# First quarter of the first feed-forward product wholly by block products, its two halves in turn, products chained in PSUM banks

## The chip, the cores and the metric

The kernel runs as one program on one core of a Trainium2 chip. The core has a matrix engine (PE in the profile, with its weight loads as PEld), a vector engine (DVE), a scalar engine (ACT), GpSimd (POOL) and a queue that issues most loads (SP). The metric is the device time of one execution in microseconds, here the median of several runs; lower is better. Fp32 products are made from three matmuls on rounded parts: each operand is split into a high part (a cast on ACT) and the rest, the low part (a subtraction on DVE), and high×high, high×low and low×high are added up in PSUM.

## The reference

One encoder layer over 512 frames of width 1024. What the change touches is the feed-forward part at its end, above all its first product, u2 (512×1024) by `w_ff1` (1024×4096):

```python
        h = h + merged @ w_out[l]
        u2 = rmsnorm(h, g_ffn[l])
        h = h + jnp.square(jax.nn.relu(u2 @ w_ff1[l])) @ w_ff2[l]
    return rmsnorm(h, g_final)
```

## The kernel before

**Tiling.** The 4096 columns of the first product are cut into four quarters of 1024, each quarter into two halves (i = 0 and 1) of 512. For each quarter the kernel makes the first product, then the part of the second product (by `w_ff2`) that it feeds, and keeps the sums in the residual tiles `hN`. The frames are cut into two blocks of 256, and the 1024 rows of `w_ff1` into two blocks of 512, so that a half is a product of 2×2 blocks.

**Block products.** Such a half is made with seven block products instead of eight (Strassen's scheme in Winograd's form, numbered 1, 2, 5, 6, 3, 7, 4 in the order of `FIRST`). A block product is 24 matmuls of 256 columns: two column groups `a`, four `k`, three parts. Its left factors are sums of blocks of u2: products 1, 2 and 4 take plain blocks; 5, 6 and 7 take three sums kept in `u2sh`/`u2sl` (high and low part, slots 0, 1 and 2), and 3 takes a sum that goes by the tiles `R7` into slot 1 of `u2h`/`u2l`. Its right factors are blocks of weights (products 1, 2, 3) or sums of blocks, `tsum` (T1 to T4), which POOL's queue writes to device memory early in the program. That queue is paced: one step of these sums goes out behind each cast of a weight chunk from the twelfth on (`next_sum`).

**The first quarter before.** Half 0 of quarter 0 is made without block products: four tiles of 128 columns, each 24 matmuls of 512 columns' worth. Tiles 0 and 1 are made by 256 frames at a time (`half`), between and behind the transposes that turn the normalized rows into u2 (`u2_turn`, for four groups of 128 frames), tiles 2 and 3 in one piece (`plain_tile`). Meanwhile `u2_sums` makes the sums of u2 blocks. Half 1 is then made with the seven block products by `first_product`. In the other quarters both halves are, one after the other.

**Buffers.** Weight chunks (128×1024, 512 KB) come through `ring`: SP loads them into `raw` (three buffers in the pool `wp` and every fourth in `yp`), `split_b` casts them to `hi` on ACT and subtracts to `lo` on DVE (three buffers each). A buffer is written again when PE has finished with what it held. Results of block products go to PSUM tiles `mm` (four banks, each 128×512), are taken out by `first_evac` into `ev` and `od` (two tiles of 128×2×512 for each half), squared after a Relu (`relu2`), and split into `ch`/`cl` (`left`), the factors of the second product.

**Order.** PE's instructions run in the order of the code. The other engines' order is set by the scheduler when the program is built; `tc.issue_after(x)` puts an instruction behind x in it. `norm_end` is the last split of u2 on DVE.

## Time and profile before

| | |
|---|---|
| median of 3 runs | 816.25 us (816.25 to 816.32) |
| the profiled execution | 815.97 us, its span 814.2 us |
| PE busy | 805.0 us, 99% of the span |
| DVE busy | 590.2 us, 72% |
| ACT busy | 438.7 us, 54% |
| mean granted PE clock | 0.998 |

The span runs from the first to the last instruction; the 1.8 us between it and the execution's time lie around it. A row of the timeline gives start, duration, engine, line, operation, the tiles written and read, and the shape; "xN" merges N like instructions, and a bracket at the end tells how long the engine was idle before and what ended that. In the windows, each engine's busy time in a stretch stands with its count of instructions, then PE's granted clock, the busy share of the DMA engines, and GB/s.

### The profile page before, as it was taken

Reading aid. Unit: us, or ns where it says so; the run is one execution under the profiler, and the core shown is the slowest. Engines: PE = TensorE matmul, PEld = TensorE weight load, DVE = VectorE, ACT = ScalarE, POOL = GpSimd, SP = SyncE. Lnnn points to the kernel's source line nnn. Section 1 sums busy time; section 2 is a strip of 40 time slices with the busy share of each in tenths; the row PEclk is TensorE's granted clock in tenths of the full one; section 3 lists DMA queues with packets and bytes.
Section 4 is the critical chain, followed back from the end, with each engine's and each line's share of the span. In section 5 each row is a group of like instructions: output and inputs, shape, how many; then the busy total and the mean of one; then the engine's idle time right before and its main releaser. Section 6 shows DMA issues by size and latency. Waiting matters only on the chain.

```text
span 814.2 us, 12430 instructions
## 1 busy us (share of the span) xinstructions
PE 805.0 (99%) x4788; PEld 707.4 (87%) x4788; DVE 590.2 (72%) x913; ACT 438.7 (54%) x694; POOL 103.9 (13%) x127
## 2 busy tenths in 40 slices
PE   9999999999999999999999999999999999999996
PEld 7788888888888888999999889988998899889984
DVE  6857877546455587877567548896788778887896
ACT  7755655443344234444454536774676367637764
POOL 0000110011101212143143000011001100100011
PEclk9999999999999999999999999999999999999999
DMA  9433666688788867757755505878658855895543
GB/s 358 172 116 131 204 165 201 188 240 246 204 250 264 230 215 190 178 151 207 205 131 159 203 1 179 261 160 216 244 165 198 218 216 166 196 253 195 156 84 124
DMA packets 38604, 155.53 MB, mean 191 GB/s; under 512 B 4560, under 2 KB 5008, under 8 KB 36496
## 3 DMA queue, kind: packets, MB, share of 16 engines
q1 hardware_dynamic: 27424, 95.98, 32.8%
q0 software_dynamic: 9328, 54.01, 31.4%
q10 hardware_dynamic: 1792, 4.75, 1.6%
q8 instruction: 37, 0.61, 0.3%
q14 instruction: 23, 0.19, 0.1%
HBM read 152.58 MB, written 31.49 MB: 226 GB/s over the span
## 4 chain that ended last, share of the span: by engine, by line
PE 96%; DVE 1%; issue 1%; DMA 0%; ACT 0%; POOL 0%; POOLq 0%; DVEq 0%; ACTq 0%
PE mm L157 24%; PE mm L158 24%; PE mm L159 24%; PE a L157 5%; PE a L158 5%; PE a L159 5%; PE mm L380 1%; PE a L394 1%; PE a L624 1%; PE a L662 1%; PE a L661 1%; DVE h L1267 1%; PE a L900 1%; PE a L408 1%; DMA mem_s<-in_memT_dram 0%
## 5 line engine op out<-in xcount | busy, mean ns | idle before, releaser
L148 DVE TENSOR_TENSOR wlo<-raw,whi 128x1024 fp32r<-128x1024 f32 x67 | 86.4, 1293 | 58.9 <-ACT whi L147 58.7
L157 PE MATMUL mm<-uhi,whi 128*128 128x512 f32 (+1 forms) x352 | 125.9, 358 | 0.0
L159 PE MATMUL mm<-uhi,wlo 128*128 128x512 f32 (+1 forms) x352 | 123.7, 351 | 0.0
L158 PE MATMUL mm<-ulo,whi 128*128 128x512 f32 (+1 forms) x352 | 123.6, 351 | 0.0
L147 ACT CAST whi<-raw 128x1024 fp32r<-128x1024 f32 x67 | 70.4, 1051 | 92.9 <-PE mm L158 56.0
L1271 ACT CAST hi<-raw 128x1024 fp32r<-128x1024 f32 x65 | 68.2, 1049 | 49.7 <-PE mm L158 32.7
L1273 DVE TENSOR_TENSOR lo<-raw,hi 128x1024 fp32r<-128x1024 f32 x65 | 79.5, 1224 | 17.6 <-ACT hi L1271 17.6
L157 PEld LDWEIGHTS mm<-uhi,whi 128*128 128x128 f32 x352 | 66.7, 189 | 9.9 <-issue 1.5
L159 PEld LDWEIGHTS mm<-uhi,wlo 128*128 128x128 f32 x352 | 66.6, 189 | 9.1
L158 PEld LDWEIGHTS mm<-ulo,whi 128*128 128x128 f32 x352 | 66.7, 189 | 8.1
L1271 ACT CAST hi<-b 128x1024 fp32r<-128x1024 f32 x40 | 41.9, 1048 | 42.0 <-PE mm L159 25.6
L158 PE MATMUL mm<-u2l,hi 128*128 128x256 f32 x224 | 63.4, 283 | 0.0
L159 PE MATMUL mm<-u2h,lo 128*128 128x256 f32 x224 | 63.4, 283 | 0.0
L157 PE MATMUL mm<-u2h,hi 128*128 128x256 f32 x224 | 63.4, 283 | 0.0
L1457 POOL DMA_DIRECT2D b<-in_wst_dram x32 | 27.3, 853 | 271.3 <-DVE lo L1273 208.1
L1273 DVE TENSOR_TENSOR lo<-b,hi 128x1024 fp32r<-128x1024 f32 x40 | 48.9, 1224 | 14.1 <-ACT hi L1271 14.0
L158 PE MATMUL mm<-lo,ch 128*128 128x512 f32 x136 | 52.9, 389 | 0.0
L157 PE MATMUL mm<-hi,ch 128*128 128x512 f32 x136 | 52.9, 389 | 0.0
L159 PE MATMUL mm<-hi,cl 128*128 128x512 f32 x136 | 52.9, 389 | 0.0
L158 PE MATMUL mm<-u2sl,hi 128*128 128x256 f32 x168 | 47.5, 283 | 0.0
L157 PE MATMUL mm<-u2sh,hi 128*128 128x256 f32 x168 | 47.5, 283 | 0.0
L159 PE MATMUL mm<-u2sh,lo 128*128 128x256 f32 x168 | 47.5, 283 | 0.0
(414 smaller groups left out, 2093.2 us busy)
## 6 DMA issues: line engine op xcount, KB each, us to landing
raw<-in_wst_dram SPq DMA_DIRECT2D x114, 512.0 KB
b<-in_wst_dram POOLq DMA_DIRECT2D x32, 512.0 KB, 5.3
raw<-T SPq DMA_DIRECT2D x28, 512.0 KB
T<-in_wst_dram POOLq DMA_DIRECT2D x12, 1024.0 KB, 9.3
b<-in_wst_dram SPq DMA_DIRECT2D x16, 512.0 KB
wb<-in_wst_dram POOLq DMA_DIRECT2D x15, 512.0 KB, 5.3
wb<-in_wst_dram SPq DMA_DIRECT2D x8, 512.0 KB
nFb<-dF ACTq DMA_DIRECT2D x6, 512.0 KB
```

The costliest lines, as they stand in the source:

```text
L147: cast = nc.scalar.copy(hi, raw)
L148: low_now[0] = nc.vector.tensor_tensor(lo, raw, f(hi), op=ALU.subtract).ins
L157: nc.tensor.matmul(ps, lh, rh, start=start, stop=False, skip_group_check=on)
L158: nc.tensor.matmul(ps, lh, rl, start=False, stop=False, skip_group_check=on)
L159: nc.tensor.matmul(ps, ll, rh, start=False, stop=stop, skip_group_check=on)
L380: nc.tensor.matmul(kps[h], w[:, h * P:(h + 1) * P], x[:, k, :], start=k == p == 0, stop=k == KT - 1 and p == 2)
L394: nc.tensor.matmul(ps, x[:, k, sl], w[low][:, kk, :], start=k == low == 0 and x is mxh, stop=k == KT - 1 and low == 1)
L408: nc.tensor.transpose(pt[:, t * P:(t + 1) * P], xn[:, t, k * P:(k + 1) * P], ident)
L624: nc.tensor.matmul(ps[e], q[a, sl], k[a, :w], start=p == 0, stop=p == 2)
L1271: nc.scalar.copy(hi, raw)
L1273: nc.vector.tensor_tensor(lo, raw, f(hi), op=ALU.subtract)
L1457: nc.gpsimd.dma_start(to[i], wst[index["B", q, i, x]], accum_op=ALU.add)
```

## The change

Half 0 of the first quarter is made with block products as well, and the two halves alternate: product 1 of half 0, of half 1, product 2 of half 0, and so on, in every quarter. I call these blocks 1a, 1b, 2a, 2b, 5a, 5b, 6a, 6b, 3a, 3b, 7a, 7b, 4a, 4b (product, then a for half 0, b for half 1). Each half has two PSUM banks, x and y. Products 1, 6, 7 and 4 are added up in x, products 2 starts y, product 5 starts it anew and 3 is added to it; the sums that DVE made one by one before are now left in PSUM, and the evacuation reads x between two products. To make the additions right, the sum of u2 for product 6 takes the other sign (and the piece `R7`, made from it, is an addition now).

1a and 2a use the two weight chunks that were loaded early for tiles 0 and 1, and stand where `half` stood; the split of u2 that only the plain tiles needed (the first 512 rows for frames 256 to 511) goes away. `first_quarter` writes out the order of splits, sums and evacuations for the start. Where it passes `low_last`, all 16 matmuls that read the high part of a chunk come first, and the eight that read the low part last. The weight sums of quarter 0 now cover both halves, so eight steps on POOL's queue move 1024 KB instead of 512 KB.

```diff
-    L += [("T", "w_ff1", P * j) for j in range(4)]
...
-    tsum = {(n, q): dram.tile([2 if q else 1, P, 1024], F32, name=f"T{n}_{q}") for q in range(4) for n in (1, 2, 3, 4)}
+    tsum = {(n, q): dram.tile([2, P, 1024], F32, name=f"T{n}_{q}") for q in range(4) for n in (1, 2, 3, 4)}
...
+        def first_mms(n, w, ps, low_last=False):
+
+            wh, wl = (t.rearrange("p (a k c) -> p a k c", a=2, k=4) for t in w)
+            (uh, ul), s = U2[n]
+
+            def mm(a, k, x, y, start, stop):
+                nc.tensor.matmul(ps[:, a, :], x[:, a, k, :], y[:, s, k, :], start=start, stop=stop, skip_group_check=True)
+
+            for low in range(1 + low_last):
+                for a in range(2):
+                    for k in range(4):
+                        if not low:
+                            mm(a, k, wh, uh, n in (1, 2, 5) and a == k == 0, False)
+                            mm(a, k, wh, ul, False, False)
+                        if low or not low_last:
+                            mm(a, k, wl, uh, False, a == 1 and k == 3)
+                        yield
...
         u2_turn(2)
-        half(0, 0)
-        half(1, 0, range(4))
+        run(first_mms(1, ws[0], banks[0][0]))
+        rest = first_mms(2, ws[1], banks[0][1])
+        run(islice(rest, 4))
         norm_end = u2_turn(3)
-        half(1, 0, range(4, KT))
-        half(0, 1)
-        half(1, 1)
+        run(rest)
...
+        def first_evac(n, i, bank, after=None):
+
+            x, y = (ps.rearrange("p a t -> p (a t)") for ps in bank)
+            (a11, a21), (a12, a22) = ([z[i][:, h, :] for h in range(2)] for z in (ev, od))
             if n == 2:
-                nc.vector.tensor_tensor(a11, a21, ps, op=ALU.add)
+                nc.scalar.copy(a11, y)
+                with tc.issue_after(after) if after is not None else ExitStack():
+                    after = add(a11, x)
                 relu2(a11)
                 left(i, 0, a11)
             if n == 5:
-                nc.scalar.copy(a22, ps)
-            if n == 6:
-                sub(a21, a21, ps)
-                sub(a22, a22, a21)
+                nc.scalar.copy(a22, y)
             if n == 3:
-                nc.vector.tensor_tensor(a12, a22, ps, op=ALU.add)
+                nc.scalar.copy(a12, y)
+                after = sub(a12, a12, x)
                 relu2(a12)
                 left(i, 1, a12)
             if n == 7:
-                sub(a22, a22, ps)
-                add(a21, ps)
+                after = sub(a22, a22, x)
                 relu2(a22)
             if n == 4:
-                add(a21, ps)
-                relu2(a21)
+                nc.scalar.activation(a21, x, AF.Relu)
+                nc.scalar.activation(a21, a21, AF.Square)
                 late_left(i)
...
+            v = first_block(0, 1, 1, B, norm_end, True)
+            with tc.issue_after(v):
+                v = sub(a22, a21, a22)
+            v = first_block(0, 2, 1, B, v, True)
+            v = parts([x[:, 0] for x in u2s], a22, v)
+            v = first_evac(2, 0, A, v)
+            v = first_block(0, 5, 0, A, v, True)
+            first_evac(5, 0, A)
+            with tc.issue_after(v):
+                sub(a21, a11, a21)
+                v = sub(a11, a22, a11)
+            v = first_evac(2, 1, B, v)
+            v = first_block(0, 5, 1, B, v, True)
+            first_evac(5, 1, B)
+            v = parts([x[:, 1] for x in u2s], a11, v)
+            v = first_block(0, 6, 0, A, v)
+            for k in range(2):
+                sl = slice(512 * k, 512 * k + 512)
+                with tc.issue_after(v):
+                    v = nc.vector.tensor_tensor(R7[k], a12[:, sl], a11[:, sl], op=ALU.add).ins
+                    v = parts([x[:, 1, 2 * k:2 * k + 2, :] for x in u2], R7[k], v)
+            v = first_block(0, 6, 1, B, v)
+            v = first_block(0, 3, 0, A, v)
...
+        def first_product(q):
+
+            pair = banks if q == 0 else banks_of()
+            done = [None] * 3 if q else first_quarter()
+            for n in FIRST[0 if q else 5:]:
+                for i, bank in enumerate(pair):
+                    first_block(q, n, i, bank, done[-3])
+                    done.append(first_evac(n, i, bank))
...
-        plain_evac(0, first[0])
-        plain_evac(1, first[1])
-        plain_tile(2)
-        u2_sums()
-        plain_tile(3)
-        load_blocks(0)
-        first_product(0, 1)
-        second_product(0)
-        for q in range(1, NQ):
-            first_product(q, 0)
-            load_blocks(q)
+        for q in range(NQ):
+            first_product(q)
...
-            first_product(q, 1)
             second_product(q)
```

Two places show how the order of the built program changes. The first is DVE's queue from the last split of u2 on. Before, the splits of the two plain tiles (`wlo`) and of block product 1 come first, then the sums of u2 blocks (`b`, `R7`) with their low parts (`u2sl`, `u2l`):

```order
L148 TENSOR_TENSOR wlo_740_4925<-raw_738_4922,whi_739_4924 128x1024
L148 TENSOR_TENSOR wlo_745_4970<-raw_743_4967,whi_744_4969 128x1024
L1273 TENSOR_TENSOR lo_750_5018<-raw_748_5015,hi_749_5017 128x1024
L1264 TENSOR_TENSOR b121_4417<-b120_4416,b121_4417 128x1024
L1264 TENSOR_TENSOR b120_4416<-b110_4414,b120_4416 128x1024
L1264 TENSOR_TENSOR b110_4414<-b110_4414,b121_4417 128x1024
```

With the change DVE has, from the chunk of 5b (`lo_749`) to that of 6b (`lo_755`):

```order
L1289 TENSOR_TENSOR lo_749_4977<-raw_747_4974,hi_748_4976 128x1024
L210 TENSOR_TENSOR cl0_4860<-ev0_4852,ch0_4858 128x512
L210 TENSOR_TENSOR u2sl_4865<-b110_4414,u2sh_4864 128x1024
L1289 TENSOR_TENSOR lo_752_5010<-raw_750_5007,hi_751_5009 128x1024
L1381 TENSOR_TENSOR R70_4862<-b111_4415,b110_4414 128x512
L210 TENSOR_TENSOR cl1_4861<-ev1_4853,ch1_4859 128x512
L210 TENSOR_TENSOR u2l_4403<-R70_4862,u2h_4402 128x512
L1381 TENSOR_TENSOR R71_4863<-b111_4415,b110_4414 128x512
L210 TENSOR_TENSOR u2l_4403<-R71_4863,u2h_4402 128x512
L1289 TENSOR_TENSOR lo_755_5046<-raw_753_5043,hi_754_5045 128x1024
```

The sums of u2 blocks now stand between the splits of weight chunks that PE takes one after the other, and the low part for 6b stands behind both pieces of `R7`.

The second place is ACT's queue in the same stretch, from the high part of 6b's chunk (`hi_754`) on. The names `u2sh` stand for two casts: the first is of the sum for product 7 (`b120`), the second for product 6 (`b110`). `hi_757` and `hi_760` are the chunks of 3a and 3b, and `hi_760` takes the buffer that `hi_751`, the chunk of 6a, had:

```order
L1287 CAST hi_754_5045<-raw_753_5043 128x1024
L209 CAST ch0_4858<-ev0_4852 128x512
L209 CAST u2sh_4864<-b120_4416 128x1024
L1328 COPY od0_4854<-mm_723_4701 128x512
L209 CAST u2sh_4864<-b110_4414 128x1024
L1302 ACTIVATE ev1_4853<-ev1_4853 128x512
L1287 CAST hi_757_5075<-raw_756_5073 128x1024
L1303 ACTIVATE ev1_4853<-ev1_4853 128x512
L1328 COPY od1_4855<-mm_725_4703 128x512
L209 CAST ch1_4859<-ev1_4853 128x512
L209 CAST u2h_4402<-R70_4862 128x512
L1287 CAST hi_760_5117<-raw_759_5115 128x1024
```

Right behind that row follows the cast of the second piece of `R7`. Before, these casts had their place while PE worked on the plain tiles, and the second piece stood ahead of the cast for the block product that follows:

```order
L210 CAST u2h_4402<-R70_4912 128x512
L1304 ACTIVATE ev0_4902<-sq_742_4953 128x2x256
L210 CAST ch0_4908<-ev0_4902 128x512
L210 CAST u2h_4402<-R71_4913 128x512
L1271 CAST hi_757_5089<-raw_756_5087 128x1024
```

So the cast of the second piece has moved from ahead of a weight chunk's cast to behind one.

More of the change, by code (lines that the diff above doesn't have):

```diff
@@ L57, in chunk_list @@
         L += [("N", "w_out", 2 * j, 512 * c) for j in range(4)]
-    L += [("T", "w_ff1", P * j) for j in range(4)]
     for q in range(4):
-        L += [(kind, q, i, b) for kind in "FB" for b in ("11", "21", "12", "22") for i in range(2) if kind == "B" or q or i]
+        L += [(kind, q, i, b) for kind in "FB" for b in ("11", "21", "12", "22") for i in range(2)]
     return L
@@ L1207, in hybrid_block @@
         run(islice(c1, 24))
-        ws = [[t.rearrange("p (k c) -> p k c", k=KT) for t in own_w(("T", "w_ff1", P * j))] for j in range(2)]
+        ws = [own_w(("F", 0, 0, b)) for b in ("11", "21")]
         def u2_turn(t):
@@ L1272, in split_b, with ring @@
             with tc.issue_after(after) if after is not None else ExitStack():
-                nc.vector.tensor_tensor(lo, raw, f(hi), op=ALU.subtract)
+                low_now[0] = nc.vector.tensor_tensor(lo, raw, f(hi), op=ALU.subtract).ins
             return hi, lo
         load_n = [0]
-        def ring(src):
+        def ring(src, after=None):
             load_n[0] += 1
@@ L1281, in ring @@
             nc.sync.dma_start(raw, src)
-            return split_b(raw)
+            return split_b(raw, after)
         def relu2(x):
@@ new lines, in first_block, with first_quarter, parts @@
+        def first_block(q, n, i, bank, after=None, low_last=False):
+            if n in (1, 2, 3):
+                src = wst[index["F", q, i, {1: "11", 2: "21", 3: "22"}[n]]]
+            else:
+                src = tsum[{5: 1, 6: 2, 7: 3, 4: 4}[n], q][i]
+            w = ring(src, after)
+            low = low_now[0]
+            run(first_mms(n, w, bank[n in (2, 5, 3)], low_last))
+            return low
+        def first_quarter():
+            (a11, a12), (a21, a22) = b11, b12
+            A, B = banks
+            def parts(pair, src, after):
+                with tc.issue_after(after):
+                    return split(*(x.rearrange("p k t -> p (k t)") for x in pair), src)
+            v = first_block(0, 1, 1, B, norm_end, True)
[21 more added lines that the diff above has]
+            v = first_block(0, 3, 0, A, v)
+            done = [first_evac(3, 0, A)]
+            v = parts([x[:, 2] for x in u2s], a21, v)
+            load_blocks(0)
+            first_block(0, 3, 1, B, v)
+            return [None, *done, first_evac(3, 1, B)]
@@ L1387, in finish @@
+        def first_product(q):
[5 more added lines that the diff above has]
+                    done.append(first_evac(n, i, bank))
+                if n == 6:
+                    load_blocks(q)
         def finish(t, c, n):
```

76 lines of the change are left out of this document (11 added, 65 removed).

## The prediction, on record before the result

> **What bounds the kernel now.** I read the page's engine shares and the shares of its chain first, then the waits of PE, then PE's timeline at the edited place, and last the other engines' windows.
>
> ```profile
> PE 805.0 (99%) x4788; PEld 707.4 (87%) x4788; DVE 590.2 (72%) x913; ACT 438.7 (54%) x694; POOL 103.9 (13%) x127
> ...
> PE 96%; DVE 1%; issue 1%; DMA 0%; ACT 0%; POOL 0%; POOLq 0%; DVEq 0%; ACTq 0%
> ...
> PE a L290 <- DVE warm L287: 1.2, 1, 1.2
> PE mm L380 <- ACT hi L274: 0.5, 1, 0.5
> ```
>
> PE is busy 99% of the span and makes 96% of the chain; its two listed waits, 1.7 us together, belong to the program's start. So a matmul less is time less, unless something makes PE wait where it now does not. Whether there is room for that is told by the first feed-forward quarter:
>
> ```profile
> 495.81 0.28 PE L157 MATMUL mm<-u2h,f2h 128*128 128x256 f32 x1
> 501.57 0.40 PE L157 MATMUL mm<-u2h,whi 128*128 128x512 f32 x1
> 512.48 0.28 PE L157 MATMUL mm<-u2h,hi 128*128 128x256 f32 x1
> 532.63 0.40 PE L157 MATMUL a<-hi,ch 128*128 128x512 f32 x1
> ...
> 500.00:550.00 50.00, 50.00 (x308) 45.12 (x307) 44.60 (x55) 36.11 (x51) 5.14 (x6) 1.00 0.82 226
> 550.00:600.00 50.00, 50.00 (x337) 46.42 (x336) 36.78 (x43) 29.04 (x38) 3.40 (x4) 1.00 0.74 216
> ```
>
> The first four rows are where the shape of the work changes: 48 matmuls of 256 columns from 495.81 (0.120 us each), 48 of 512 from 501.57 (0.227), then the seven block products of half 1, 168 matmuls, in 20.15 us (0.120 again), and the second product at 532.63. These intervals are back to back. In the windows the fourth number is DVE: 44.6 of 50 us in the stretch with this quarter, against 36.8 in the next. DVE is close to full exactly where the change takes PE work away.
>
> **What is removed.** Half 0 had four tiles: 96 matmuls of 256 columns and 48 of 512, of which the first 48 of 256 columns stand ahead of 495.81 and are the same count for 1a and 2a. From 495.81 to 532.63 PE needed 36.82 us. Now twelve blocks of 24 matmuls remain from there (1b, 2b, 5a to 4b): 288 x 0.120 = 34.55 us. Without waits the change gains 2.27 us, 0.28%. Elsewhere PE's matmuls are the same.
>
> **What it adds in waits.** I follow DVE and ACT row by row in the built order, with these durations:
>
> ```profile
> 494.15 1.07 ACT L210 CAST u2h<-a 128x512 fp32r<-128x512 f32 x2 [1.09 <-PE a L1214]
> 498.89 0.60 ACT L1303 ACTIVATE sq<-mm 128x512 f32<-128x512 f32 x1 [2.22 <-PE mm L159]
> 502.27 1.04 ACT L210 CAST u2sh<-b 128x1024 fp32r<-128x1024 f32 x1
> 503.20 0.64 ACT L1304 ACTIVATE ev<-sq 128x512 f32<-128x512 f32 x1
> ...
> 495.97 2.35 DVE L148 TENSOR_TENSOR wlo<-raw,whi 128x1024 fp32r<-128x1024 f32 x2
> 499.37 3.74 DVE L1264 TENSOR_TENSOR b<-b,b 128x1024 f32<-128x1024 f32 x3
> 503.15 0.69 DVE L1264 TENSOR_TENSOR R<-b,b 128x512 f32<-128x512 f32 x1
> 503.76 1.22 DVE L211 TENSOR_TENSOR u2sl<-b,u2sh 128x1024 fp32r<-128x1024 f32 x1
> ...
> 793.90 1.28 DVE L1267 TENSOR_TENSOR h<-h,a 128x512 f32<-128x512 f32 x2
> 795.33 0.47 PE L157 MATMUL a<-hi,ch 128*128 128x512 f32 x1
> ```
>
> On DVE an operation of 1024 columns takes 1.22 us and the next starts 1.13 after it started (two in 2.35); one of 512 takes 0.69, the next follows after 0.61 (503.15 to 503.76). On ACT these are 1.05 and 0.95, 0.60 and 0.50. ACT starts on a finished bank 0.2 us after PE's next block starts (498.89; PE's block began at 498.69, 24 matmuls after 495.81). Another engine's result is taken up after 0.04; PE goes on 0.15 after a result it waits for (DVE ends at 795.18, PE starts at 795.33).
>
> *A floor by DVE alone.* In the new order DVE has, from the low part of 1b's chunk to that of 6b's, 11 operations of 1024 columns and 8 of 512: 11 x 1.13 + 8 x 0.61 = 17.3 us. It can start at 495.9 (before, at 495.97), so 6b's low part is there at 513.3 at best. Unhindered, PE wants it at 6b's third matmul, 495.81 + 5 x 2.88 + 0.24 = 510.45. With 0.15 to start that is 3.0 us of waiting even if DVE never waits, more than the gain. In the kernel before, DVE did its sums under 10.9 us of plain tiles that need none.
>
> *With the waits of the two queues.* Up to 5a PE has room: 1b's low part is needed at its seventeenth matmul, 497.73, and done at 497.1; 2b's at 500.61, done at 499.5; 5a's sum at 501.7, done at 500.7. DVE's first sum starts only at 497.15, since ACT copies 2a's bank (496.01) before the block of u2 it needs.
> - **5b.** Its low part stands behind two sums and an addition: DVE starts it at 505.37, done 506.58; wanted at 504.45 + 16 x 0.12 = 506.37. PE waits 0.4.
> - **6a.** ACT goes through hi of 6b (503.69, when 5a has let its buffer go), `ch` 504.64, the cast for product 7 at 505.14, a bank copy 506.09, and only at 506.59 the cast that 6a needs, done 507.64. DVE follows with `u2sl` (507.68 to 508.90) and 6a's low part (508.81 to 510.03). 6a, due at 507.33 and 0.4 late, gets to its third matmul at 510.18: 2.2 more.
> - **6b.** `hi_760` takes 6a's buffer, so ACT stands still until 6a is through (512.86), casts it from 512.90 and then the second piece of `R7` (513.85 to 514.45). Queued behind that on DVE are `u2l` (514.49) and 6b's low part (515.10 to 516.32). PE, at 6b since 512.82, waits at its third matmul until 516.47: 3.4.
>
> That is 0.4 + 2.2 + 3.4 = 6.0 us. Behind 6b each block of 2.88 us asks DVE for one split and about one operation of 512 columns (1.74), so it runs ahead again; products 3, 7, 4 follow without a gap.
>
> *The bank handovers.* In every quarter 7a may write x only after it was subtracted for product 3: behind 3a one cast that stands ahead on ACT (0.12 + 0.95), the copy of y (0.60), the subtraction (0.04 + 0.69), and 0.15 to start, 2.55 us, under 3b's 2.88. 5 after 2 has no subtraction, 4 after 7 no copy: shorter. No cost; 0.33 us of cover, and what is over that would count eight times. If such a step came 1 us late each time, 5 us.
>
> *Loads.* Four `raw` buffers turn as before, and a load is issued when the split four chunks earlier is done.
>
> ```profile
> 493.78 0.33 SPq L1504 DMA_DIRECT2D gl<-in_gfin_dram  x1
> ...
> 495.00:497.00 2.00, 1.00 0.81 236
> 497.00:498.00 1.00, 1.00 0.00 0
> ...
> L131 POOL DMA_DIRECT2D T<-in_wst_dram x16: 774/825/862, 96.1 to 306.6; - x16
> ...
> 80.00:140.00 60.00, 5.45 (x8) 1.00 0.62 186
> ...
> 200.00:300.00 100.00, 100.00 (x565) 84.29 (x565) 58.91 (x107) 39.42 (x76) 13.81 (x22) 1.00 0.80 234
> ```
>
> The load issued at 493.78 moved its 512 KB by 497.0, when the DMA engines fall silent: 3.2 us. With that, no cast above waits for data (6a's chunk is asked for at 497.2 and cast at 500.81). At 6 us each the three stalls would grow to about 8. The `gl` load still stands ahead of the ring in SP's queue and goes out when the norm ends, as before. The wider weight sums of quarter 0 run on POOL's queue around 85 to 140, where the DMA engines are 62% busy; from 200 to 300, with sums of full size at 80%, PE still was busy throughout. I cost them at nothing, between 0 and 1 us.
>
> Sum against the profiled execution: 815.97 - 2.27 + 6.0 = 819.7; its 815.97 is 0.28 under the median, which gives **820.0 us**.
>
> **Rivals.**
> - *The waits don't come* and PE stays gapless, because the engines turn out faster or ordered otherwise: 816.25 - 2.3 = 814.0. For it speaks that PE had no gap in this whole part; against it, DVE's 17.3 us, which no order of ACT shortens.
> - *DVE's floor alone*: ACT delivers in time and only the 3.0 us remain: 816.25 + 0.7 = 817.0. That needs 6a's cast some 1.3 us earlier and the `R7` cast not behind `hi_760`, which the order contradicts.
> - *PE's clock drops.* The wait inside 6b is about as long as the one after which the clock falls at the end of the program:
>
> ```profile
> 806.00:807.00 1.00, 0.79 (x4) 1.00 0.00 0
> ...
> 810.00:811.00 1.00, 0.00 (x0) 0.66 0.06 25
> 811.00:812.00 1.00, 0.00 (x0) 0.50 0.98 389
> ```
>
>   PE's last matmul ends at 806.79, the granted clock is 0.66 on average over 810 to 811 and then 0.50, so it fell 3.9 us after. A gap of 3.4 us modelled, a little longer in fact, would set it off; 6b's remaining 22 matmuls at 0.24 us instead of 0.12 cost 2.6 us: 822.6. The Trainium skill ("TensorE: Matmul & The Clock Gate", "What's actually happening") has the clock halve after an idle window of about 3.4 us and come back after as long a busy one; by that rule this rival is a toss-up, and the row's 3.9 us leans against it.
> - *Late loads or handovers*: loads that land in 6 us (stalls of 8 us, as above), or handovers 0.25 us over their cover, eight times. Either is some 2 us on top, 822. For it speaks the thin cover; against it, that the casts above have their data 0.3 us and more ahead.
>
> **How the numbers follow.** Forecast (waits of 6 us, half a microsecond either way and more) 54%; DVE's floor 12%; clock drop 13%; late loads or handovers 9%; no waits 12%. The range takes from DVE's floor to the clock drop, 816.9 to 822.6. A change counts from 0.2%, 1.6 us, which is about what a measurement of this kernel tells from none. Faster is the case without waits, with a gain of 2.3: 0.12. The floor, +0.7, is no change: 0.12. The rest is slower: 0.76.
>
> **What would show it.** Rows of PE waits that read nothing in this part before should name DVE's `lo` and `u2sl` in 5b, 6a and 6b, longest about 3.4, at 506 to 517 us, and none from 3a on or in later quarters. The second product should start at 536.4 rather than 532.63, and the matmul count fall by 48 of 512 columns and rise by 72 of 256. I am wrong if 6b's low part is ready before 513.3, if `u2l` from the second `R7` piece is not what it waits behind, or if gaps stand at 7a or 4a in each quarter.

## The result, and the profile after

The change makes the kernel slower: 827.93 us (median of 5 runs, 826.29 to 829.99) beside 816.28 us of the kernel before on the same chip (816.25 to 818.19). The ratio is 1.0139, 95% interval 1.0119 to 1.0159. The direction was forecast; the size was not: the prediction said 820.0 us, with 822.6 as its upper end.

The profiled execution took 829.99 us, its span is 828.2 us: it is the longest of the five, so what its profile shows is read below as that execution's loss and not as the median's. The engine shares of its page, its chain, and the list of PE's waits (sum, count, longest) answer to the lines that the prediction opened with:

```profile
PE 810.6 (98%) x4812; PEld 711.0 (86%) x4812; DVE 574.9 (69%) x889; ACT 442.9 (53%) x705; POOL 104.1 (13%) x127
...
PE 90%; DVE 4%; ACT 2%; DMA 2%; issue 1%; POOL 0%; POOLq 0%; DVEq 0%; ACTq 0%
...
PE mm L1228 <- DVE lo L1289: 3.6, 2, 2.9
PE a L661 <- DVE PTl L210: 1.9, 1, 1.9
...
PE mm L1228 <- ACT u2sh L209: 1.0, 1, 1.0
PE mm L1228 <- DVE u2sl L210: 0.9, 1, 0.9
PE mm L158 <- DVE cl L210: 0.8, 1, 0.8
```

The matmul count rose by 24, which is 72 of 256 columns more and 48 of 512 fewer. Yet PE is busy 5.6 us longer, although it has 2.27 us less work at full clock: some of its matmuls ran at a lower clock. Three of the waits (`lo`, `u2sh`, `u2sl` at L1228) stand in the first quarter, where they were forecast. Two others were not forecast at all: `PTl` at L661 belongs to the FoX stage near 135 us (one of the attention branches, early in the program), `cl` at L158 to the last second product near 800 us.

Where the time went is read from the first matmul of each stage, taken from the timeline of PE, the kernel before first:

```profile
489.12 0.36 PE L157 MATMUL mm<-u2h,f2h 128*128 128x256 f32 x1
570.74 0.28 PE L157 MATMUL mm<-u2h,hi 128*128 128x256 f32 x1
767.89 0.40 PE L157 MATMUL a<-hi,ch 128*128 128x512 f32 x1
806.41 0.39 PE L159 MATMUL a<-hi,cl 128*128 128x512 f32 x1
```

and the changed kernel:

```profile
494.13 0.36 PE L1228 MATMUL mm<-u2h,f2h 128*128 128x256 f32 x1
544.96 0.40 PE L156 MATMUL a<-hi,ch 128*128 128x512 f32 x1
583.07 0.28 PE L1228 MATMUL mm<-u2h,hi 128*128 128x256 f32 x1
780.22 0.40 PE L156 MATMUL a<-hi,ch 128*128 128x512 f32 x1
820.59 0.39 PE L158 MATMUL a<-hi,cl 128*128 128x512 f32 x1
```

The rows are block product 1's first matmul, the second product of quarter 0 (532.63 before), the first product of quarter 1, the second product of quarter 3, and the last matmul. The differences give four stretches:

| stretch | before | after | difference |
|---|---|---|---|
| up to block product 1 | 489.12 | 494.13 | +5.01 |
| first product of quarter 0 | 43.51 | 50.83 | +7.32 |
| from there to the last second product | 235.26 | 235.26 | 0.00 |
| last second product | 38.52 | 40.37 | +1.85 |

Their sum is 14.18 us; the two profiled executions differ by 14.02.

**The first product of quarter 0.** The timeline of PE, from the end of 5b to the end of 6b (the bracket is the idle time before a row and what ended it):

```profile
511.27 0.28 PE L1228 MATMUL mm<-u2sl,hi 128*128 128x256 f32 x1
511.61 1.21 PE L1228 MATMUL mm<-u2sh,lo 128*128 128x256 f32 x8
513.80 0.38 PE L1228 MATMUL mm<-u2sh,hi 128*128 128x256 f32 x1 [0.98 <-ACT u2sh L209]
515.07 0.38 PE L1228 MATMUL mm<-u2sl,hi 128*128 128x256 f32 x1 [0.88 <-DVE u2sl L210]
516.20 0.38 PE L1228 MATMUL mm<-u2sh,lo 128*128 128x256 f32 x1 [0.75 <-DVE lo L1289]
...
517.61 0.41 PE L1228 MATMUL mm<-u2sl,hi 128*128 128x256 f32 x1
...
520.16 0.41 PE L1228 MATMUL mm<-u2sl,hi 128*128 128x256 f32 x1
523.45 0.39 PE L1228 MATMUL mm<-u2sh,lo 128*128 128x256 f32 x1 [2.87 <-DVE lo L1289]
...
524.39 0.37 PE L1228 MATMUL mm<-u2sh,hi 128*128 128x256 f32 x1
...
527.93 0.28 PE L1228 MATMUL mm<-u2h,lo 128*128 128x256 f32 x1
```

Measured from start to start, less the usual 0.12 us, the waits are 0.22 (5b), 1.14 + 1.15 + 1.01 (the first three matmuls of 6a; the last of 5b's eight low matmuls starts at 512.54, the end of its row less 0.28) and 3.17 (6b): 6.69 us. Besides, twelve intervals from 517.61 to 520.16 took 2.55 us and seventeen from 524.39 to 527.93 took 3.54, where 0.12 each would be 1.44 and 2.04; with 0.1 for each of three slow first matmuls behind a wait that is 2.9 us. The sum closes: -2.27 + 6.69 + 2.9 = +7.3.

What 6b waited for is seen on the other two engines, first ACT, then DVE:

```profile
519.98 1.04 ACT L1287 CAST hi<-raw 128x1024 fp32r<-128x1024 f32 x1 [2.57 <-PE mm L1228]
520.93 0.61 ACT L209 CAST u2h<-R 128x512 fp32r<-128x512 f32 x1
```

```profile
521.57 0.69 DVE L210 TENSOR_TENSOR u2l<-R,u2h 128x512 fp32r<-128x512 f32 x1 [2.84 <-ACT u2h L209]
522.18 2.35 DVE L1289 TENSOR_TENSOR lo<-raw,hi 128x1024 fp32r<-128x1024 f32 x2
```

This is the forecast's queue, link by link: the cast of 3b's chunk (`hi_760`) stands still until 6a lets its buffer go, the cast of the second `R7` piece stands behind it, `u2l` waits for that cast, and 6b's low part is behind `u2l`. For 6a there was one link more than forecast: the cast of 6b's chunk, which stands ahead on ACT, waited for its load.

```profile
509.81 1.05 ACT L1287 CAST hi<-raw 128x1024 fp32r<-128x1024 f32 x1 [1.24 <-DMA raw<-T]
```

**Up to block product 1.** In the FoX stage DVE takes up a load named `nFb`. The rows of DVE for it, before and after:

```profile
127.57 0.76 DVE L607 TENSOR_TENSOR nFb<-nFb,cst_s 128x128 f32<-128x128 f32 x2 [0.84 <-DMA nFb<-dF]
```

```profile
133.29 0.76 DVE L606 TENSOR_TENSOR nFb<-nFb,cst_s 128x128 f32<-128x128 f32 x2 [4.88 <-DMA nFb<-dF]
```

It is taken up 5.7 us later. ACT's queue had issued the first of the two loads at 124.38 instead of 123.42, so most of the 5.7 us passed between the issue and the take-up. The chain that ended last runs through this load: 8.88 us from 124.38, then `nFb`, a split of weights and `PTl` on DVE, then PE at 137.24. PE is 0.3 us behind the kernel before from its first 10 us on, 1.0 from 113 us, 3.0 at 137.24, where `PTl` is late, and 5.0 at 142; the last part is its clock. So about 4.7 of the 5.0 us belong to the FoX stage. The windows around it (the number after POOL's count is the granted clock, then the DMA share), one of the kernel before and three of the changed kernel:

```profile
100.00:120.00 20.00, 20.00 (x118) 17.01 (x119) 14.90 (x39) 11.83 (x25) 1.69 (x3) 1.00 0.65 188
```

```profile
100.00:120.00 20.00, 20.00 (x109) 16.40 (x109) 14.78 (x40) 11.48 (x26) 1.34 (x2) 1.00 0.92 271
...
135.00:140.00 5.00, 3.10 (x17) 2.43 (x15) 4.97 (x8) 2.43 (x4) 0.81 (x1) 0.87 0.34 108
140.00:145.00 5.00, 5.00 (x21) 3.94 (x22) 2.55 (x5) 1.05 (x3) 0.00 (x0) 0.79 0.95 176
```

The DMA engines were 65% busy from 100 to 120 us before, and are 92% busy now.

**The last second product.** A low part of a left factor (`cl`) is late, at the first slot of half 1 (the interval is 1.04 us over the usual 0.23; the rest of the 1.85 us lies in smaller delays):

```profile
799.94 0.49 PE L157 MATMUL mm<-lo,ch 128*128 128x512 f32 x1
801.21 0.50 PE L158 MATMUL mm<-hi,cl 128*128 128x512 f32 x1 [0.77 <-DVE cl L210]
```

### The profile page after: what moved, and what is told of

Read it like the earlier page. It is cut to its first block, busy times and chain, and to the rows that moved or that the text cites. A ratio compares the mean times of both kernels' runs of the same rounds, so it can differ in the third digit from the quotient of the medians.

```text
span 828.2 us, 12463 instructions
## 1 busy us (share of the span) xinstructions
PE 810.6 (98%) x4812; PEld 711.0 (86%) x4812; DVE 574.9 (69%) x889; ACT 442.9 (53%) x705; POOL 104.1 (13%) x127
## 4 chain that ended last, share of the span: by engine, by line
PE 90%; DVE 4%; ACT 2%; DMA 2%; issue 1%; POOL 0%; POOLq 0%; DVEq 0%; ACTq 0%
PE mm L1228 18%; PE mm L156 16%; PE mm L157 16%; PE mm L158 16%; PE a L157 5%; PE a L156 5%; PE a L158 5%; DVE lo L1289 2%; PE mm L379 1%; PE a L393 1%; DMA nFb<-dF 1%; PE a L661 1%; DVE h L1283 1%; PE a L899 1%; PE a L407 1%
## 5 line engine op out<-in xcount | busy, mean ns | idle before, releaser
L147 DVE TENSOR_TENSOR wlo<-raw,whi 128x1024 fp32r<-128x1024 f32 x65 | 84.7, 1306 | 58.2 <-ACT whi L146 58.2
L158 PE MATMUL mm<-uhi,wlo 128*128 128x512 f32 (+1 forms) x352 | 123.9, 352 | 0.0
L146 ACT CAST whi<-raw 128x1024 fp32r<-128x1024 f32 x65 | 68.4, 1052 | 90.3 <-PE mm L157 54.9
L1287 ACT CAST hi<-raw 128x1024 fp32r<-128x1024 f32 x70 | 73.4, 1048 | 60.2 <-PE mm L1228 42.8
L1289 DVE TENSOR_TENSOR lo<-raw,hi 128x1024 fp32r<-128x1024 f32 x70 | 85.3, 1220 | 28.3 <-ACT hi L1287 28.3
L158 PEld LDWEIGHTS mm<-uhi,wlo 128*128 128x128 f32 x352 | 66.7, 190 | 9.2
L1228 PE MATMUL mm<-u2h,hi 128*128 128x256 f32 x240 | 67.4, 283 | 0.0
L1228 PE MATMUL mm<-u2l,hi 128*128 128x256 f32 x240 | 67.4, 283 | 0.0
L1228 PE MATMUL mm<-u2h,lo 128*128 128x256 f32 x240 | 65.6, 283 | 0.0
L1228 PE MATMUL mm<-u2sh,lo 128*128 128x256 f32 x192 | 53.5, 291 | 3.7 <-DVE lo L1289 3.6
L1228 PE MATMUL mm<-u2sl,hi 128*128 128x256 f32 x192 | 55.1, 290 | 0.9 <-DVE u2sl L210 0.9
L1228 PE MATMUL mm<-u2sh,hi 128*128 128x256 f32 x192 | 55.0, 290 | 1.0 <-ACT u2sh L209 1.0
L158 PE MATMUL mm<-hi,cl 128*128 128x512 f32 x136 | 53.1, 390 | 0.8 <-DVE cl L210 0.8
```

The lines of the kernel that those rows point to most:

```text
L146: cast = nc.scalar.copy(hi, raw)
L147: low_now[0] = nc.vector.tensor_tensor(lo, raw, f(hi), op=ALU.subtract).ins
L158: nc.tensor.matmul(ps, ll, rh, start=False, stop=stop, skip_group_check=on)
L1228: nc.tensor.matmul(ps[:, a, :], x[:, a, k, :], y[:, s, k, :], start=start, stop=stop, skip_group_check=True)
L1287: nc.scalar.copy(hi, raw)
L1289: low_now[0] = nc.vector.tensor_tensor(lo, raw, f(hi), op=ALU.subtract).ins
```

## The experiments

Each kernel ran beside the kernel before on the same chip; e1 to e4, e5 to e7, e8 and e9, and e10 are four such groups, in which the kernel before took 816.28, 816.52, 816.32 and 816.47 us. For those that compute in another order the table gives the same stretches as above, from their profiled executions: how late block product 1 starts against 489.12, then the lengths of quarter 0's first product (43.51 before), of its second product (38.11 before and in the change), and of the last second product.

| kernel | median us (range) | start | first product | second product | last |
|---|---|---|---|---|---|
| changed | 827.93 (826.29 to 829.99) | +5.01 | 50.83 | 38.11 | 40.37 |
| e1 | 843.7 (840.55 to 845.23) | +18.44 | 51.72 | 38.11 | 40.35 |
| e2 | 818.11 (817.63 to 821.77) | +1.81 | 43.52 | 38.10 | 38.53 |
| e3 | 824.8 (821.89 to 826.4) | +4.64 | 47.48 | 38.10 | 40.40 |
| e4 | 818.16 (818.04 to 819.71) | +1.89 | 43.51 | 38.11 | 40.37 |
| e5 | 826.78 (826.03 to 828.76) | +0.91 | 51.43 | 38.11 | 40.38 |
| e6 | 822.05 (820.98 to 824.15) | +0.96 | 42.79 | 42.60 | 40.35 |
| e7 | 820.49 (820.1 to 823.53) | +3.56 | 42.94 | 42.61 | 38.56 |
| e8 | 821.78 (821.04 to 822.04) | +1.46 | 43.45 | 42.36 | 38.54 |
| e9 | 821.78 (821.18 to 825.35) | +5.41 | 43.37 | 42.33 | 38.56 |
| e10 | 819.78 (817.06 to 821.49) | +0.70 | 43.86 | 38.11 | 38.53 |

In the profiles of e1, e3 and e4 PE's matmuls from 6 to about 9.5 us run at half their pace (e4 has 10 in the window 6 to 8 us where the kernel before has 19), and PE is 1.8 to 2.1 us late by 10 us; the granted clock of these windows still reads 1.00. It has nothing to do with the change: e4's +1.89 is that. The kernel before has executions at 818 us too, 1.8 above its others; none of them was profiled, so that they are the same is not shown.

**e1 and e2: the weight sums.** e1 is the changed kernel with quarter 0's sums as in the kernel before and half 0's sums at the very end of the list:

```diff
-        for q in range(4):
+        for q, h in ((0, slice(1, 2)), (1, slice(0, 2)), (2, slice(0, 2)), (3, slice(0, 2)), (0, slice(0, 1))):
```

> The changed kernel, but the weight sums of quarter 0 are made for half 1 first, as before, and for half 0 last of all, behind those of the other quarters; so around 85 to 140 us the steps on POOL's queue move 512 KB again. Theory: the wider steps delay the load of nFb, by which DVE and then PE waited at 134 to 141 us (PE 4.7 us behind the kernel before there). Then the transposes of the last rows stand at about 493.5 to 494 us instead of 498.5, no PE wait is listed there, and the time falls by 4 to 5 us, to about 823. Rival: the early shift has another cause (chance of the run, other addresses): PE is still 3 us or more behind at 141 us, and the time stays near 828.

Measured: 843.7 us, ratio 1.0327 (1.0301 to 1.0352), a miss by 20 us. The waits of its profile tell why:

```profile
ACT whi L146 <- DMA wb<-in_wst_dram: 39.5, 8, 12.3
...
PE mm L156 <- ACT whi L146: 7.9, 2, 6.2
```

Half 0's steps now stand at 315 to 360 us on POOL's queue, between the accumulating loads of `wb` for the gate stage, each of which is awaited by a cast (15.7 us in all before, none over 3.8). What was to relieve one stage stopped the next, and the time says nothing of the FoX stage. The profile does: between 10 and 250 us PE falls 0.9 us further behind the kernel before, where the changed kernel's falls 4.7, and the wait for `nFb` near 131 us is 1.6 us instead of 4.88.

e2 is the kernel before with nothing but the wide sums:

```diff
-                i = index["F", q, 0 if q else 1, src] if isinstance(src, str) else None
-                yield tsum[n, q], tsum[src, q] if i is None else wst[i:i + (2 if q else 1)], add
+                i = index["F", q, 0, src] if isinstance(src, str) else None
+                yield tsum[n, q], tsum[src, q] if i is None else wst[i:i + 2], add
```

> The kernel before, with nothing changed but the weight sums of quarter 0, which cover both halves (1024 KB steps; the sums of half 0 are not used). Theory: these steps alone bring the early wait: 819 to 821 us, PE behind by 3 to 5 us from about 140 us on, and the rest as before. Rival: the wider steps are hidden under PE's work: 816.3 within 0.5.

Measured: 818.11 us, ratio 1.0032 (1.0018 to 1.0046); single executions reach 821.8. Its profiled execution, at 817.78 one of the shorter ones, has the wait of DVE for `nFb` at 7.1 us in three, 3.5 the longest, where the kernel before has

```profile
DVE nFb L607 <- DMA nFb<-dF: 4.0, 3, 2.5
```

Its +1.81 arises there, 1.0 us at 112 and the rest at 134 us; at the start it loses nothing. So the wide steps alone cost 1.8 us in the median, and more in some executions; less than the changed kernel's profile shows, and less than the 819 to 821 us that were expected. A wide step is wider and twice the bytes at once; e2 doesn't part the two.

**e3: 6b's low part first.** One line is moved: in the changed kernel 6b's split stands ahead of both `R7` pieces.

```diff
+            v = first_block(0, 6, 1, B, v)
             for k in range(2):
...
-            v = first_block(0, 6, 1, B, v)
```

> The changed kernel, but on DVE the low part of 6b's chunk stands ahead of the two pieces of R7 and their low parts. Theory (6b waits for what is queued ahead on DVE, which itself waits for ACT behind the buffer of 6a): the 3.2 us wait in 6b goes to 0.3 or less, 3a waits 0.5 to 1 instead, the second stretch of half clock (about 1.8 us) goes too; 823 to 824.5 us. Rival (DVE's sum of work alone counts): the wait only moves on to 3a, 2.5 us or more there, and the time stays within 1.5 us of the change.

Measured: 824.8 us, ratio 1.0096 (1.0072 to 1.0120). Its list of PE's waits has `lo` at 0.7 and no longer at 2.9:

```profile
PE mm L1228 <- DVE u2sl L210: 0.9, 1, 0.9
PE mm L1228 <- ACT u2sh L209: 0.9, 1, 0.9
...
PE mm L1228 <- DVE lo L1289: 0.7, 1, 0.7
```

The 0.7 is 6a's; the wait inside 6b is gone, and it did not move on to 3a. The first product is 3.35 us shorter, about that wait (3.17). The clock's share did not shrink with it, as had been expected: PE ran at half clock from 514 to 521 us without a break, behind 6a's waits alone. That 6b waits behind the second `R7` piece is shown; the order of two lines was worth 3 us, about as much as forecast for the wait.

**e4: the later quarters alone.** The kernel before in quarter 0 and in the sums; quarters 1 to 3 in turn and chained in banks.

```diff
-            first_product(q, 0)
-            load_blocks(q)
+            chain_product(q)
...
-            first_product(q, 1)
```

> The kernel before in quarter 0 and in its weight sums; quarters 1 to 3 have the halves in turn and the products chained in PSUM banks as in the change. Theory: the handovers of the banks cost nothing (quarters of 78.4 us as before), and only the last quarter loses 1 to 2 us, where the low parts of both halves' left factors pile up on DVE: 817.5 to 818.3 us. Rival: the handovers cost in each quarter, 819 or more; or nothing anywhere, 816.3.

Measured: 818.16 us, ratio 1.0022 (1.0012 to 1.0031). In the profile the last second product takes 40.37 us, as in the changed kernel, and the `cl` wait of 0.8 us is there; quarters 1 and 2 cost nothing. The 1.85 us come with the halves made in turn and chained in the last quarter; e4 changes both at once, so which of the two it is stays open.

**e5: early narrow sums.** The changed kernel with quarter 0's sums as 512 KB steps, begun eight weight chunks earlier.

```diff
-        for q in range(4):
+        for q, h in ((0, slice(0, 1)), (0, slice(1, 2)), (1, slice(0, 2)), (2, slice(0, 2)), (3, slice(0, 2))):
...
-        op = next(sums, None) if n > 11 else None
+        op = next(sums, None) if n > 3 else None
```

> The changed kernel, with quarter 0's weight sums as separate 512 KB steps for each half (all of half 0, then all of half 1), begun 8 chunks of weights earlier, so that the FoX stage again sees narrow steps and half 1's are behind it in time. Theory (the first 5.0 us are lost because wide steps crowd out the load that nFb waits for): nFb is taken up within 3 us of its neighbours' pace again, PE's shift at the transposes of the last rows falls from +5.0 to between 0 and +1.5 us, and the time from 827.9 to 823 to 826. Rival (the early loss is not from the width of the steps but from something else that the change moved, or from the volume alone): the shift stays at +4 us or more and the time at 827 to 829. What can spoil it: steps brought forward to 30 to 85 us may meet the first weight loads there, which would show as new waits of PE before 85 us.

Measured: 826.78 us, ratio 1.0127 (1.0108 to 1.0146). In the profiled execution the FoX stage is back to the pace of before,

```profile
128.32 0.76 DVE L606 TENSOR_TENSOR nFb<-nFb,cst_s 128x128 f32<-128x128 f32 x2 [0.66 <-DMA nFb<-dF]
```

and block product 1 starts 0.91 us late instead of 5.01. The time was to fall to between 823 and 826 us and follows only by 1.15 us, so it missed that; the two kernels' intervals overlap. The profile's gain and the median's differ because the profiled execution of the changed kernel was the longest of its five. With 7.32 and 1.85 for the other two places, the median's 11.65 us leave 2.5 for the early part, an estimate by subtraction (1.6 to 1.9 with the first product of e1 or e5, which took 8.2 and 7.9 us more than before). How much is lost changes from execution to execution, and the steps begun early have a price of their own (e7 shows it).

**e6 and e7: taking out the waits.** In e6, half 0's and half 1's product 4, which need only a plain block of u2, are made right behind 2b into two banks of their own, copied by ACT and added behind product 7; e3's line is in it too. e7 adds e5's sums and makes quarters 1 to 3 half by half as before.

```diff
+            Z = [at_([P, 2, 256]) for _ in range(2)]
+            v = first_block(0, 4, 0, Z, v, True, True)
+            nc.scalar.copy(ev[0][:, 1, :], Z[0].rearrange("p a t -> p (a t)"))
...
+            v = first_block(0, 4, 1, Z[1:], v, True, True)
+            nc.scalar.copy(ev[1][:, 1, :], Z[1].rearrange("p a t -> p (a t)"))
...
             if n == 7:
                 after = sub(a22, a22, x)
+                if q == 0:
+                    after = add(a21, x)
                 relu2(a22)
+                if q == 0:
+                    relu2(a21)
+                    late_left(i)
```

> The changed kernel, with quarter 0's product 4 made right behind 2b into two banks of its own (it needs only a plain block of u2, no sum), copied to the second half of the result, and added in behind product 7; and 6b's low part put ahead of the two R7 pieces on DVE. Weight sums and later quarters as in the change. Theory (the first quarter loses 6.8 us by DVE and ACT queues that are 3 us behind PE, and some 2.8 us by the clock falling with those waits): 5.76 us of PE work that asks nothing of DVE but two splits covers the queue, the waits named lo, u2sl and u2sh go from 7.5 us to under 0.5, the granted clock stays at 1.00 there, the region from the second half of 2a to the second product falls from 45.6 us to about 36.1 to 37, and the time from 827.9 to 818.3 to 820. Rival (the waits move to 7a or to 4's copies, or the clock falls for another reason): region 39 us or more, time 822 or more.

> All three causes taken out at once: product 4 early in quarter 0, quarter 0's weight sums as early narrow steps, and quarters 1 to 3 half by half as in the kernel before (only the sign of sum 6 differs). If the three causes are the whole story, what is left is the gain that the shape change alone has: 816.3 - 2.27 = 814.0, between 813.5 and 815. Rival (a cause was missed, or the gain of 2.27 us is itself not there): 816 or more.

Measured: e6 822.05 us (ratio 1.0068, 1.0042 to 1.0093), e7 820.49 us (1.0057, 1.0038 to 1.0076). The first half of the theory holds: in e6 the first product takes 42.79 us, 8.0 less than in the change and 0.7 less than before. But the second product behind it grew from 38.11 to 42.60 us, in e7 likewise. The row of PE in e6 with the longest wait in that stretch:

```profile
555.15 0.79 PE L158 MATMUL mm<-hi,cl 128*128 128x512 f32 x1 [1.56 <-DVE cl L210]
```

and its windows (the fourth number is DVE):

```profile
540.00:550.00 10.00, 9.74 (x44) 7.76 (x43) 10.00 (x15) 7.56 (x12) 1.71 (x2) 1.00 0.73 154
550.00:560.00 10.00, 8.24 (x27) 6.06 (x28) 7.57 (x10) 3.03 (x4) 1.71 (x2) 0.83 0.83 195
```

DVE is busy without a break from 540 to 550. The product that asks it for little had stood at the end, where it covered the late left factors; moved ahead it covers the sums and uncovers the factors. (Made early, product 4 also costs DVE one more addition of 512 columns for each half, which is part of it.) "The three causes are the whole story" fell: there is a fourth, hidden in the change by the order it had. e7's last second product is 38.56 us, so half by half, unchained, does away with the 1.85. Its start is 3.56 us late in the profile; PE waited 2.2 us for `V` at 77 us, and DVE, which makes `V`, had stood for an earlier load of the same kind:

```profile
75.37 0.76 DVE L606 TENSOR_TENSOR nFb<-nFb,cst_s 128x128 f32<-128x128 f32 x2 [3.74 <-DMA nFb<-dF]
```

In the kernel before no weight sum ran at that time; here a step of 512 KB was issued at 62.27. This load was late for another reason than the one near 130 us: it reads back `dF`, and SP issued it at 69.56 instead of 64.96, since it waited up to 4.5 us for the 4 KB writes of `dF` (0.4 before). e5, e8 and e10, with the same early steps, issued it at 68.6 to 68.8 and lost less. So it isn't the width of the steps alone; that this step held up the writes is read from the times, not tried.

**e8 and e9: six additions to POOL.** e8 is e7 with the two `R7` additions and the four subtractions of late left factors in quarter 0 on POOL instead of DVE; e9 is e8 with the change's wide sums.

```diff
+                nc.gpsimd.tensor_tensor(R7[k], a12[:, sl], a11[:, sl], op=ALU.add)
...
-                    v = nc.vector.tensor_tensor(R7[k], a12[:, sl], a11[:, sl], op=ALU.add).ins
...
-                    late_left(i)
+                    late_left(i, nc.gpsimd)
```

> The kernel of e7 with six additions of 512 columns moved from DVE to POOL in quarter 0: the two R7 sums and the four subtractions behind product 4 that make the left factors of slots 2 and 3. Theory (what e7 still loses, 1.1 us at product 3's low part and 1.6 us and a clock drop in the second product, is DVE running behind by its sheer load): 1.2 us less on DVE ahead of product 3 and 2.4 us less ahead of the second product's later factors take both waits away; the second product of quarter 0 takes 42.6 us in e6 and about 38.1 here, and the time falls from 820.5 to between 814.5 and 816.5. Rival (POOL's additions, 1.6 us each where DVE needs 0.69, come too late themselves or slow DVE down): the second product stays above 41 us and the time at 819 or more.

> The kernel of e8 with the change's own weight sums (wide steps of quarter 0, begun at chunk 12). Theory (the wide steps delay the load of nFb, by an amount that differs between executions): slower than e8 by 1 to 3 us, with a wider spread of the runs, 815.5 to 819, and a wait of DVE for nFb of 3 us or more in the profile where e8 shows about 1. Rival (the early narrow steps cost as much elsewhere): within 0.7 us of e8.

Measured: both 821.78 us; e8's ratio is 1.0059 (1.0046 to 1.0072), e9's 1.0067 (1.0051 to 1.0083). The rival of e8 came true: the second product still takes 42.36 us. In the first product a row of DVE in e8, and the row of POOL that overlaps it, show what the move costs:

```profile
507.93 3.97 DVE L1289 TENSOR_TENSOR lo<-raw,hi 128x1024 fp32r<-128x1024 f32 x2
```

```profile
506.45 4.37 POOL L1381 TENSOR_TENSOR R<-b,b 128x512 f32<-128x512 f32 x2 [12.81 <-DVE b L1280]
```

POOL needs 2.2 us for an addition that takes DVE 0.69, and two splits that took 2.35 us together take 3.97 while POOL adds: DVE gave back 1.6 us of what it was spared. In the second product DVE now waits for POOL as well, and the subtraction behind that takes 1.78 us instead of 0.68:

```profile
541.61 1.78 DVE L1283 TENSOR_TENSOR od<-od,s 128x512 f32<-128x512 f32 x1 [1.18 <-POOL s L1312]
```

PE's two waits there, 2.0 us for a low part and 1.6 for `cl`, follow behind it. The Trainium skill ("GPSIMD Engine Reference", "Key points") says that POOL shares its SBUF interfaces with DVE and contends with DVE instructions that read two SBUF inputs; the rows of both products agree, and put a number on it. In e9's profile `nFb` waits 5.5 us and block product 1 starts 5.41 late, where e8 has 1.7 and 1.46. In the profiles wide is worse by 4 us, but e9's profiled execution is the longest of its six; in the medians the two are equal, as e9's rival had it, so over all executions it is open which kind of sums costs more.

**e10: half the cover at each end.** e7 with only 4a made early; 4b stays last.

```diff
-            v = first_block(0, 4, 1, Z[1:], v, True, True)
-            nc.scalar.copy(ev[1][:, 1, :], Z[1].rearrange("p a t -> p (a t)"))
...
             for n in FIRST[0 if q else 5:]:
                 for i, bank in enumerate(pair):
+                    if (q, n, i) == (0, 4, 0):
+                        continue
```

> The kernel of e7 with only half 0's product 4 made early (2.88 us of cover ahead of 5a), half 1's left last as in the change (2.88 us of cover for half 0's late left factors). Theory (DVE's work from 495 to 555 us nearly fills it, so that the cover of 5.76 us is missed wherever it isn't: all behind in the change, 6.8 us of waits ahead; all ahead in e6 and e7, 4.5 us lost in the second product): split, the first quarter waits 0.5 to 2.5 us and the second product is back at 38.1 to 39.5 us; from e7's 820.5 the time falls to 815.5 to 818. Rival (the two places are not one account, the second product's loss comes from product 7's longer way out): the second product stays at 41 us or more for either half and the time at 819 to 821.

Measured: 819.78 us (817.06 to 821.49, 11 runs), ratio 1.0034 (1.0021 to 1.0046). The second product is back at 38.11 us (533.68 to 571.79). The first product takes 43.86, 0.35 more than before, with two waits left:

```profile
PE mm L1228 <- DVE od L1280: 1.3, 1, 1.3
...
PE mm L1228 <- DVE lo L1289: 0.5, 1, 0.5
```

That the second product comes back at all is what the rival denied, though the median lies in the rival's 819 to 821 us. The stages agree with the theory that the two places are one account of DVE's time. The profiled execution, the shortest, is 0.6 to 0.8 us above the kernel before; the median is 2.7 above that execution. The range expected for the time ended at 818, so it was missed. Where the longer executions lose it no profile here shows; the early stages, where e7 and e9 lost 3.6 and 5.4 us, are the likely place, but it isn't shown. No version beat the kernel before.

## Why the prediction was wrong

The median came 7.9 us above the forecast. The steps that failed are three that the sum puts at nothing: the weight sums (some 2.5 us of the median by subtraction, 4.7 in the profile), the clock beside the waits (2.9 us), and the last quarter (1.85 us). The waits that the sum is made of were short by 0.7. Point by point, by its own steps:

- **The gain of 2.27 us: right.** The blocks run at 0.12 us a matmul wherever they don't wait, and the account of the first product closes with -2.27.
- **The waits in the first product, 6.0 us: right in place and cause, 0.7 short.** 5b 0.22 for 0.4, 6b 3.17 for 3.4, 6a 3.30 for 2.2. The missing part is 6a: the cast of 6b's chunk waited 1.24 us for its load, where the text said that no cast above waits for data. e3 shows 6b's queue to be the cause.
- **The clock: right as a mechanism, wrong as an alternative.** The rival priced 2.6 us with a chance of 13%. It came on top of the waits, 2.9 us in two pieces, and the first piece followed the three waits of 6a, which the rival did not consider; in e3, where 6b doesn't wait, they set it off by themselves. The reading that 3.9 us of idleness are needed, from the program's end, did not hold for a stretch that is only half idle.
- **The handovers of banks and quarters 1 and 2: right.** 235.26 us before and after.
- **The weight sums, "at nothing, between 0 and 1 us": the largest miss in the profile.** The FoX stage lost 4.7 us in the profiled execution; e2, with the wide sums alone, lost 1.8 in the median. The row cited for it (PE busy throughout from 200 to 300 us with the DMA engines 80% busy) was from a stage in which only POOL's queue waits for a transfer. At 85 to 140 us DVE waits for one, `nFb`; that wait, 4.0 us in three, stood in the trace of before, and the prediction left it out. e5 and e9 tie the late `nFb` to the wide steps in their profiles: near 130 us it waits 0.7 and 5.5 us.
- **Later quarters at no cost: wrong in the last.** +1.85 us. In DVE's rows the late left factors of both halves come together at the end, with the final norm's work beside them. e4 and e7 show that halves in turn and chained make it and that half by half and unchained does not; turn and chain were not separated, and that DVE's load is the reason is read from its rows, not tried by itself.
- **The start of the second product, 536.4: it came at 544.96.** Of the 8.6 us, 5.0 come from the stages ahead (4.7 from the FoX stage), 0.7 from the waits, 2.9 from the clock.

Beside the miss in size, one thing was not seen at all: that a stage's cover works at both ends. The change put blocks that each need a split of their chunk in 2.88 us where there had been 10.9 us of plain tiles that need two splits and no sum, and none of the orders tried in e6 to e10 had room for all of it: in the change PE waits at 510 us, in e6 and e7 at 555, and e10, in between, still has 1.8 us of waits. It isn't that DVE has more to do: it is busy 35.2 us in the first product with the change and 36.5 before.

## What to carry to other kernels

When PE is 99% busy, a change that saves matmuls takes away the cover of a second engine's work, and is paid where that engine is nearly full: add up its work over the whole stage and the next one, not only up to the first deadline. A transfer that lies beside other work is not free because PE stays busy under heavier traffic elsewhere; look for the loads on the critical chain in the stage where it falls, with the longest wait for them. Price the clock together with the waits, as a chance: several waits of a microsecond close together halved it here in all four profiles that have them, while single waits of about 2 us did so in some and not in others.

## What the runs showed of the hardware

- **The clock falls sooner than a single idle gap suggests.** The windows of the changed kernel:

```profile
512.00:514.00 2.00, 1.02 (x8) 0.80 (x7) 0.37 (x2) 2.00 (x4) 0.01 (x1) 1.00 0.75 225
514.00:516.00 2.00, 0.57 (x2) 0.19 (x1) 2.00 (x2) 2.00 (x4) 0.87 (x1) 1.00 0.88 227
516.00:518.00 2.00, 1.80 (x13) 1.80 (x14) 1.97 (x4) 1.37 (x3) 0.00 (x0) 0.90 0.88 139
518.00:520.00 2.00, 2.00 (x12) 2.00 (x11) 0.73 (x2) 0.02 (x1) 0.00 (x0) 0.50 1.01 303
```

  No gap was longer than 1.2 us, PE was busy 1.59 of 4 us, and the clock fell 1.4 us after PE was at work again. 6a's waits did the same in e1, e3 and e5. In the FoX stage one wait of 1.9 us was enough (0.87 and 0.79 in the windows shown above), and 1.6 us in the second product of e6 and e7; but 2.2 us at 77 us in e7 and 2.0 us at 550 us in e8 left the granted clock at 1.00. So the length of a wait alone does not decide it. The Trainium skill ("TensorE: Matmul & The Clock Gate", "What's actually happening") has the clock halve after an idle window of about 3.4 us, in windows that run freely; the rows agree with a window of that kind only if a half-idle one counts as idle.
- **A load was later beside wider transfers, by a varying amount.** At 128 to 134 us `nFb`, 512 KB, was taken up after a wait of 0.7 to 1.7 us in the seven profiles with 512 KB steps there and of 3.1 to 5.5 in the five with 1024 KB steps. At 75 us in e7 DVE waited 3.7 us for it, because SP issued it 4.6 us later: the small writes that it reads back were late. The runs spread with it: 4.1 us between the shortest and the longest of e2, beside 2.1 for the kernel before in the same runs.
- **POOL and DVE slow each other.** Two splits of 1024 columns took 3.97 us beside POOL's additions instead of 2.35, and POOL's additions 2.2 us each.
